# Rows of the second norm moved from GpSimd to VectorE, the exponentials' table loaded earlier, the routing weights computed last

## The chip, the cores and the metric

The kernel runs on one core of one Trainium2 chip. The metric is the device time of one execution in microseconds (us); lower is better. The times shown are the median of several runs, with the lowest and highest.

## What is computed

Two layers of a transformer-like block over 256 latent tokens and 256 context tokens of width 1024, in float32. Each layer runs three token mixers, merges and projects them, and adds the result to the stream. Then comes a second RMS norm with a modulation (a scale and a shift per row kind), a router over 16 experts in 4 groups that picks two experts of one group for each token, and a mixture of gated experts. The first layer keeps context and latents (512 tokens), the second only the latents (256). Cut to the part around the change:

```python
def modulate(h, shift, scale):
    return h * (1 + scale) + shift

mix = token_mixers(h, ...)                      # ends with  merged @ w_out
x = x + m[2] * mix
hx = modulate(rms_norm(x, norm2), m[3], m[4])   # the second norm's rows
probs = softmax(hx @ w_router)
sel = probs + b_router                          # choose group, then two experts
wts = probs[chosen] / sum(probs[chosen])        # the choices' weights
x = x + m[5] * sum(wts * expert(hx))
```

## The kernel before

Each layer is `mixers` followed by `tail` (line 986). `tail` has three stretches.

**Output projection** (`output_projection`, line 903). The merged tiles are split into a rounded high part `mh` (ScalarE, line 913) and the rest `ml` (VectorE, line 914), and each piece of the weights `w_out` into `whi` (ScalarE, line 231) and `wlo` (VectorE, line 232). TensorE makes three matmuls for each block, high by high, high by low, low by high (lines 243 to 245). There are four token tiles of 128 in layer 0 and two in layer 1, and two column halves of 512. `done` evicts a result: times the gate `m2` into `tm` (VectorE, line 921), then added to `x` (line 922). `vectors` (line 1053) issues, from ScalarE's queue behind the last `mh`, the DMAs of the router and the modulation: in layer 0 the 2 MB `m34`, in layer 1 the small `mc8`. `loaded` (line 1067) turns these into what the router needs (columns `mcol`, scaled router `wrm`, bias `blg` by matmuls at line 1081) and scales them: `m34` at line 1087 in layer 0, `mc8` at line 1084 in layer 1.

**Norm and routing.** `tile_done(t)` (line 1091) follows each tile: transposes (line 1098) to `h2T`, the square sum (ScalarE, line 1101), the reciprocal root `rsx` (VectorE and GpSimd, lines 295 and 296), the router's logits (line 1106, `lg` at line 1127). In layer 0 it also makes the norm's rows `xg`: scaled by ScalarE (line 1108), multiplied and shifted by GpSimd in two halves (lines 1111 and 1112), written to `h2d` in DRAM by SyncE's queue (line 1113). In layer 1 it makes a high part `hh` (ScalarE, line 1118) and a low part `hl` of the scaled rows, for tile 0 on VectorE (line 1120) and for tile 1 on GpSimd (lines 1123 and 1124). After each pair of tiles `route` (line 1221) runs: maximum `mx` (line 1228), exponentials `pr` with a load of ScalarE's table (line 1230), reciprocal (line 1233), selection scores `se` (line 1235), the choice of two experts by some twenty small VectorE operations up to `ohb` (line 1267), ranks by matmul (`rnk`, line 1275). What it returns, `weights` (lines 1289 to 1298), makes the normalized weights `wts` and `comb`; it is called last in `tile_done`.

**Placing and experts.** In layer 0 `place_tiles` (line 1302) and `indices` (line 1325) find which row goes to which slot (`M`, `cc`, `gix`, `six`); a gather on GpSimd's queue (line 1371) then reads the rows back from `h2d`, TensorE transposes them (line 1402), and `xh` and `xl` (lines 1403 and 1404) are the first expert's input. In layer 1 `place_group` (line 1339) builds placing masks `Mg` (line 1344), multiplies `hh` and `hl` by them on TensorE (line 1352) and the weights onto the masks (`MW`, line 1363).

The program's text gives dependencies; the order in which each engine issues is set by a scheduler with a cost model, which `tc.issue_after` and `tc.high_priority` steer. So code moved in one place can reorder instructions elsewhere. Every engine issues in its order, one behind the other.

Of the kernel before, what the change touches and what calls it, by code (L numbers as in the profile page):

```python
# [12 lines left out]
F32 = mybir.dt.float32  # L13
# [5 lines left out]
AF = mybir.ActivationFunctionType  # L19
ALU = mybir.AluOpType  # L20
AX = mybir.AxisListType
PSUM = bass.MemoryType.PSUM

D = 1024
NT = 4
# [6 lines left out]
CIDN, CUTR, CIOT, CNCM, CZER, CWAM, CCOS, CSIN, CGD, CED, CPID, CEND = (  # L32
    0, 128, 256, 384, 448, 704, 1216, 1344, 1472, 1476, 1492, 1496)
# [34 lines left out]
def mk(ap, off, dims):  # L68
    return bass.AP(tensor=ap.tensor, offset=ap.offset + off, ap=[list(ap.ap[0])] + [list(d) for d in dims])
# [7 lines left out]
def kernel(es, tc, A, out, dbg=None):  # L77
    nc = tc.nc
    V, S, G, PE, SY = nc.vector, nc.scalar, nc.gpsimd, nc.tensor, nc.sync
# [7 lines left out]
    sm = es.enter_context(tc.tile_pool(name="sm", bufs=2))  # L87
# [38 lines left out]
    C = cst.tile([128, CEND], F32, name="C")  # L126
# [3 lines left out]
    nhalf = cst.tile([128, 8], F32, name="nhalf")  # L130
# [68 lines left out]
    def later():  # L199

        return tc.issue_after(loads[-1].ins)
# [701 lines left out]
    def output_projection(l, op, mg, x, vectors, loaded, tile_done):  # L903

        full = l == 0
        nt = 4 if full else 2
# [4 lines left out]
        for k in range(8):  # L911
            m = mg[k // 4][:, k % 4]
            last = S.copy(mh[:, k], m)
            V.tensor_tensor(ml[:, k], m, mh.bitcast(F32)[:, k], ALU.subtract)

        vectors(last)

        def done(t, dh, ps):
            cs = slice(512 * dh, 512 * dh + 512)
            tm = op.tile([128, 512], F32, name="tm", bufs=2)  # L920
            V.tensor_tensor(tm, ps, m2[:, 1 if full and t < 2 else 0, cs], ALU.mult)
            (V if dh else G).tensor_tensor(x[:, t, cs], x[:, t, cs], tm, ALU.add)
# [59 lines left out]
    h2d = [tc.dram_tile([512, D], F32, name="h2d0")]  # L982
# [3 lines left out]
    def tail(l, mp, mgp, mg, side, other):  # L986


        full = l == 0
        nt = 4 if full else 2  # L990
# [4 lines left out]
        x = xp.__enter__().tile([128, nt, D], F32, name="x")  # L995
# [9 lines left out]
        with ExitStack() as ms, ExitStack() as ps_:  # L1005
            mo = ms.enter_context(tc.tile_pool(name=f"mo{l}", bufs=1, side=side))
            br = mo.tile([128, 16], F32, name="br")
            S.dma_start(br, A["b_router"].partition_broadcast(128))
            utr = mo.tile([128, 128], BF16, name="utr")
            G.tensor_copy(utr, C[:, CUTR:CUTR + 128])  # L1010
            one = mo.tile([128, 128], BF16, name="one")
# [20 lines left out]
            with ExitStack() as rs_:  # L1032
# [17 lines left out]

                lgs, placed = [None], None

# [38 lines left out]
                def tile_done(t):  # L1091
# [13 lines left out]
                    for k in range(8):  # L1105
                        PE.matmul(lg, hT[:, k], wrm[:, r, k], start=k == 0, stop=k == 7)
                    if full:
                        S.activation(xn, x[:, t], AF.Copy, scale=rs)
                        for g in range(2):
                            cs = slice(512 * g, 512 * g + 512)  # L1110
                            G.tensor_tensor(xn[:, cs], xn[:, cs], m34[:, r, 1, cs], ALU.mult)
                            G.tensor_tensor(xn[:, cs], xn[:, cs], m34[:, r, 0, cs], ALU.add)
                        SY.dma_start(h2d[l][128 * t:128 * (t + 1)], xn)
                    else:

                        xk = mk(x, D * t, [[1, 8], [8, 128]])
                        blocks = lambda a: a.rearrange("p (k i) -> p k i", k=8)
                        S.activation(blocks(hh[:, t]), xk, AF.Copy, scale=rs)
                        if t < nt - 1:
                            V.scalar_tensor_tensor(blocks(hl_[:, t]), xk, rs, blocks(hh.bitcast(F32)[:, t]),  # L1120
                                                   ALU.mult, ALU.subtract)
                        else:
                            G.tensor_scalar(blocks(xn), xk, rs, None, ALU.mult)
                            G.tensor_tensor(hl_[:, t], xn, hh.bitcast(F32)[:, t], ALU.subtract)
                    if t % 2 == 0:
                        lgs[0] = rp.tile([128, 2, 16], F32, name="lg", bufs=2)
                    V.scalar_tensor_tensor(lgs[0][:, t % 2], lg, rs, blg[:, r], ALU.mult, ALU.add)
                    if t % 2 == 0:
                        return
                    later = route(rp, lgs[0], t, nt, br, wts, comb, ohb, rnk, rnb if full else None, rhs, utr, one, cnt)  # L1130
                    if full:
                        nonlocal placed
                        placed = place_tiles(rp, (t - 1, t), cap, iot, rnb, rhs, cc, None if t < nt - 1 else
                                    lambda g: indices(rp, cc, gix, six, g))
                    later()

# [15 lines left out]
                if not full:  # L1152
# [7 lines left out]
                    def place(g):  # L1160
                        if g < 4:
                            for a, r in zip((xT, WT), place_group(g, rp, p2, nt, rnk, comb, hh, hl_, mc8)):
                                a.append(r)
# [56 lines left out]

    def route(rp, lg, t1, NT_, br, wts, comb, ohb, rnk, rnb, rhs, utr, one, cnt):

# [4 lines left out]
        bc = lambda x, n, k=1: mk(x, 0, [[k, 2], [0, n]])  # L1227
        V.tensor_reduce(mx, lg, AX.X, ALU.max, negate=True)
        for i in range(2):
            S.activation(pr[:, i], lg[:, i], AF.Exp, bias=mx[:, i:i + 1], accum_out=sm_[:, i:i + 1])  # L1230
        if t1 == NT_ - 1:
# [34 lines left out]
        V.tensor_tensor(o2, e, bc(v, 16), ALU.is_equal)  # L1266
        V.tensor_tensor(ohb[:, t0:t0 + 2], o1, o2, ALU.add)

# [69 lines left out]

    def place_group(g, rp, xp_, nt, rnk, comb, hh, hl_, mc8):

        M = rp.tile([128, nt, 4, 64], F32R, name="Mg", bufs=2)
        xT = xp_.tile([128, 8, 256], F32, name="xT", bufs=2)
        for t in range(nt):
            V.tensor_tensor(M[:, t], mk(C, CIOT, [[0, 4], [1, 64]]), mk(rnk, 16 * t + 4 * g, [[1, 4], [0, 64]]),
                            ALU.is_equal)
        for k2 in range(4):
# [371 lines left out]
```

## Time and profile before

| what | value |
|---|---|
| median of 3 runs | 1770.28 us (1768.99 to 1772.41) |
| the profiled execution | 1766.91 us |
| its span, first to last instruction | 1764.8 us |
| mean granted TensorE clock | 0.976 of full |
| TensorE busy | 1653.8 us, 94% of the span |
| VectorE busy | 1049.4 us, 59% |
| ScalarE busy | 818.7 us, 46% |
| GpSimd busy | 346.2 us, 20% |

Times in the profile count from the span's start. PE is TensorE, DVE VectorE, ACT ScalarE, POOL GpSimd, SP SyncE; a "q" behind a name is the engine's sequencer or queue. A timeline row gives start and duration, engine, line, operation, output and inputs; the bracket at its end is the time that the engine stood idle before it and what ended that. PEclk is the granted clock, 1.00 being the upper of its two levels (2.4 GHz) and 0.50 the lower (1.2 GHz).

### The profile page before, as it was taken

Reading aid. Unit: us, or ns where it says so; the run is one execution under the profiler, and the core shown is the slowest. Engines: PE = TensorE matmul, PEld = TensorE weight load, DVE = VectorE, ACT = ScalarE, POOL = GpSimd, SP = SyncE. Lnnn points to the kernel's source line nnn. Section 1 sums busy time; section 2 is a strip of 40 time slices with the busy share of each in tenths; the row PEclk is TensorE's granted clock in tenths of the full one; section 3 lists DMA queues with packets and bytes.
Section 4 is the critical chain, followed back from the end, with each engine's and each line's share of the span. In section 5 each row is a group of like instructions: output and inputs, shape, how many; then the busy total and the mean of one; then the engine's idle time right before and its main releaser. Section 6 shows DMA issues by size and latency. Waiting matters only on the chain. (4 is left out here: it accounts for less than half of the span.)

```text
span 1764.8 us, 24182 instructions
## 1 busy us (share of the span) xinstructions
PE 1653.8 (94%) x8912; PEld 1218.6 (69%) x8913; DVE 1049.4 (59%) x1908; ACT 818.7 (46%) x1353; POOL 346.2 (20%) x343
## 2 busy tenths in 40 slices
PE   8999999999999999589999996999999999699998
PEld 4657677887677788477877774878887888443333
DVE  4328482447867335688888889488548786411101
ACT  3313232336676442368778774444446875301100
POOL 0003040222300123411221104143213202100000
PEclk9999999999999999799999997999999999899999
DMA  9895747523211355499999962322524345899996
GB/s 289 295 321 175 245 168 257 183 73 96 60 49 36 101 183 196 170 315 368 369 328 364 363 237 86 113 79 60 191 82 105 105 120 204 342 413 414 412 378 269
DMA packets 235312, 380.02 MB, mean 215 GB/s; under 512 B 33447, under 2 KB 130215, under 8 KB 225585
## 3 DMA queue, kind: packets, MB, share of 16 engines
q1 hardware_dynamic: 223248, 361.19, 59.1%
q10 hardware_dynamic: 7616, 9.43, 1.6%
q0 software_dynamic: 4320, 7.75, 1.3%
q8 instruction: 74, 1.21, 0.3%
q14 instruction: 54, 0.43, 0.1%
HBM read 370.50 MB, written 17.72 MB: 220 GB/s over the span
## 5 line engine op out<-in xcount | busy, mean ns | idle before, releaser
L232 DVE TENSOR_TENSOR wlo<-wraw,whi 128x1024 fp32r<-128x1024 f32 (+2 forms) x368 | 438.6, 1212 | 176.1 <-ACT whi L231 161.6
L231 ACT CAST whi<-wraw 128x1024 fp32r<-128x1024 f32 (+2 forms) x368 | 369.4, 1023 | 171.1 <-PE psg L245 77.2
L243 PE MATMUL psg<-hTh,whi 128*128 128x512 f32 (+1 forms) x576 | 206.6, 360 | 0.0
L244 PE MATMUL psg<-hTl,whi 128*128 128x512 f32 (+1 forms) x576 | 205.4, 357 | 0.0
L245 PE MATMUL psg<-hTh,wlo 128*128 128x512 f32 (+1 forms) x576 | 204.2, 356 | 0.0
L243 PE MATMUL psg<-whi,hTh 128*128 128x512 f32 (+1 forms) x392 | 148.6, 383 | 2.2 <-ACT hTh L373 2.1
L244 PE MATMUL psg<-wlo,hTh 128*128 128x512 f32 (+1 forms) x392 | 148.1, 379 | 0.0
L245 PE MATMUL psg<-whi,hTl 128*128 128x512 f32 (+1 forms) x392 | 147.3, 379 | 0.5 <-DVE hTl L404 0.4
L243 PEld LDWEIGHTS psg<-hTh,whi 128*128 128x128 f32 x576 | 109.1, 190 | 27.1 <-issue 10.1
L245 PEld LDWEIGHTS psg<-hTh,wlo 128*128 128x128 f32 x576 | 109.0, 190 | 19.0 <-issue 6.1
L244 PEld LDWEIGHTS psg<-hTl,whi 128*128 128x128 f32 x576 | 109.3, 190 | 16.0 <-issue 4.0
L1478 PE MATMUL psg<-wraw,xT 128*64 128x512 f32 x512 | 113.2, 595 | 2.9 <-PEq L1149 2.7
L243 PE MATMUL psg<-whi,xh 128*128 128x512 f32 x256 | 101.8, 398 | 0.7 <-ACT xh L1403 0.7
L244 PE MATMUL psg<-wlo,xh 128*128 128x512 f32 x256 | 100.0, 391 | 0.0
L245 PE MATMUL psg<-whi,xl 128*128 128x512 f32 x256 | 99.6, 390 | 0.0
L243 PEld LDWEIGHTS psg<-whi,hTh 128*128 128x128 f32 x392 | 74.3, 190 | 19.5 <-ACT hTh L373 3.8
L1478 PEld LDWEIGHTS psg<-wraw,xT 128*64 128x64 f32 x512 | 35.9, 137 | 74.4 <-issue 72.2
L245 PEld LDWEIGHTS psg<-whi,hTl 128*128 128x128 f32 x392 | 73.9, 189 | 16.8 <-DVE hTl L404 1.7
L244 PEld LDWEIGHTS psg<-wlo,hTh 128*128 128x128 f32 x392 | 74.4, 190 | 13.3 <-issue 0.5
L587 ACT ACTIVATE P<-P,smx 128x512 f32<-128x512 f32 (+1 forms) x96 | 62.2, 648 | 22.9 <-DVE smx L586 20.4
L836 POOL TENSOR_TENSOR mg<-mg,gates 128x512 f32<-128x512 f32 (+1 forms) x32 | 38.1, 1198 | 172.1 <-DVE gates L835 126.2
L1371 POOL DMA_INDIRECT xg<-h2d,gix x16 | 27.8, 1739 | 204.5 <-PE pst L1402 188.5
(414 smaller groups left out, 3256.9 us busy)
## 6 DMA issues: line engine op xcount, KB each, us to landing
wraw<-in_w_down_dram SPq DMA_DIRECT2D x64, 1024.0 KB
wraw<-in_w_ada_dram SPq DMA_DIRECT2D x40, 1024.0 KB
wraw<-in_w_in_dram SPq DMA_DIRECT2D x144, 256.0 KB
wraw<-in_w_up_dram SPq DMA_DIRECT2D x32, 1024.0 KB
wraw<-in_w_gate_dram SPq DMA_DIRECT2D x32, 1024.0 KB
wraw<-in_w_gate_dram SPq DMA_DIRECT2D x64, 512.0 KB
wraw<-in_w_up_dram SPq DMA_DIRECT2D x64, 512.0 KB
wraw<-in_w_in_dram SPq DMA_DIRECT2D x24, 1024.0 KB
```

Source lines behind the costliest of these rows:

```text
L231: S.copy(hi[:, :, 0:n], r[:, 2 * j:2 * j + 2, 0:n])
L232: V.tensor_tensor(lo[:, :, 0:n], r[:, 2 * j:2 * j + 2, 0:n], hi.bitcast(F32)[:, :, 0:n], ALU.subtract)
L243: PE.matmul(ps, ah, bh, start=start, stop=False)
L244: PE.matmul(ps, ah, bl, start=False, stop=False)
L245: PE.matmul(ps, al, bh, start=False, stop=stop)
L587: S.activation(flat, flat, AF.Exp, scale=-1.0, bias=m[:, 0:1], accum_out=m[:, 2:3])
L836: G.tensor_tensor(dst, dst, sg[:, i], ALU.add)
L1371: return G.indirect_dma_start(out=xg, out_offset=None, in_=h2d[l][:, :], in_offset=bass.IndirectOffsetOnAxis(ap=idx, axis=0), bounds_check ...
L1478: PE.matmul(pgu[64 * c:64 * c + 64, :], xT[:, 2 * p + k, o:o + 64], r[:, :, k, 256 * c:256 * c + 256], start=p == 0 and k == 0, stop=p == ...
```

## The change

- ScalarE runs one `Exp` on a small tile behind the last `mh` cast of each output projection, so that the table is loaded there (lines 918 and 919 of the changed kernel).
- Layer 0's rows are made on VectorE in two operations of 128x1024: `rows_a` (line 1123) scales by `rsx` and multiplies by `m34`, `rows_b` (line 1131) adds the shift and issues the write. ScalarE's copy and the GpSimd operations are gone. For the last tile `rows_a` is issued behind the maximum, `rows_b` behind the choice.
- In layer 1, for tile 1, GpSimd keeps the scaled rows (now into `xn` first), ScalarE copies them to `hh` behind the exponentials (line 1127), and VectorE subtracts behind the choice (line 1137).
- `weights` runs last: in layer 0 behind the indices, in layer 1 behind the first placing masks.

```diff
@@ output_projection
         vectors(last)
 
+        with tc.issue_after(last.ins):
+            S.activation(sm.tile([128, 8], F32, name="warm"), nhalf, AF.Exp)
+
@@ tail
+                def weigh(after):
+
+                    with tc.issue_after(after.ins):
+                        while weights:
+                            weights.pop(0)()
@@ tile_done
-                    if full:
-                        S.activation(xn, x[:, t], AF.Copy, scale=rs)
-                        for g in range(2):
-                            cs = slice(512 * g, 512 * g + 512)
-                            G.tensor_tensor(xn[:, cs], xn[:, cs], m34[:, r, 1, cs], ALU.mult)
-                            G.tensor_tensor(xn[:, cs], xn[:, cs], m34[:, r, 0, cs], ALU.add)
-                        SY.dma_start(h2d[l][128 * t:128 * (t + 1)], xn)
-                    else:
-
-                        xk = mk(x, D * t, [[1, 8], [8, 128]])
-                        blocks = lambda a: a.rearrange("p (k i) -> p k i", k=8)
-                        S.activation(blocks(hh[:, t]), xk, AF.Copy, scale=rs)
-                        if t < nt - 1:
+
+                    xk = mk(x, D * t, [[1, 8], [8, 128]])
+                    blocks = lambda a: a.rearrange("p (k i) -> p k i", k=8)
+
+                    def rows_a():
+
+                        if full:
+                            V.scalar_tensor_tensor(xn, x[:, t], rs, m34[:, r, 1], ALU.mult, ALU.mult)
+                        elif t < nt - 1:
+                            S.activation(blocks(hh[:, t]), xk, AF.Copy, scale=rs)
+                        else:
+                            S.copy(hh[:, t], xn)
+
+                    def rows_b():
+                        if full:
+                            V.tensor_tensor(xn, xn, m34[:, r, 0], ALU.add)
+                            SY.dma_start(h2d[l][128 * t:128 * (t + 1)], xn)
+                        elif t < nt - 1:
                             V.scalar_tensor_tensor(blocks(hl_[:, t]), xk, rs, blocks(hh.bitcast(F32)[:, t]),
                                                    ALU.mult, ALU.subtract)
                         else:
-                            G.tensor_scalar(blocks(xn), xk, rs, None, ALU.mult)
-                            G.tensor_tensor(hl_[:, t], xn, hh.bitcast(F32)[:, t], ALU.subtract)
+                            V.tensor_tensor(hl_[:, t], xn, hh.bitcast(F32)[:, t], ALU.subtract)
+
+                    if t < nt - 1:
+                        rows_a()
+                        rows_b()
+                    elif not full:
+                        G.tensor_scalar(blocks(xn), xk, rs, None, ALU.mult)
...
-                    later = route(rp, lgs[0], t, nt, br, wts, comb, ohb, rnk, rnb if full else None, rhs, utr, one, cnt)
+                    weights.append(route(rp, lgs[0], t, nt, br, wts, comb, ohb, rnk, rnb if full else None, rhs, utr, one,
+                                         cnt, (rows_a, rows_b) if t == nt - 1 else None))
                     if full:
                         nonlocal placed
                         placed = place_tiles(rp, (t - 1, t), cap, iot, rnb, rhs, cc, None if t < nt - 1 else
                                     lambda g: indices(rp, cc, gix, six, g))
-                    later()
+                    if full and t == nt - 1:
+                        weigh(placed)
@@ route
-        V.tensor_reduce(mx, lg, AX.X, ALU.max, negate=True)
+        first = V.tensor_reduce(mx, lg, AX.X, ALU.max, negate=True)
         for i in range(2):
-            S.activation(pr[:, i], lg[:, i], AF.Exp, bias=mx[:, i:i + 1], accum_out=sm_[:, i:i + 1])
+            second = S.activation(pr[:, i], lg[:, i], AF.Exp, bias=mx[:, i:i + 1], accum_out=sm_[:, i:i + 1])
+        if meanwhile:
+            with tc.issue_after((first if NT_ == NT else second).ins):
+                meanwhile[0]()
...
-        V.tensor_tensor(ohb[:, t0:t0 + 2], o1, o2, ALU.add)
+        chosen = V.tensor_tensor(ohb[:, t0:t0 + 2], o1, o2, ALU.add)
+        if meanwhile:
+            with tc.issue_after(chosen.ins):
+                meanwhile[1]()
@@ place_group
         for t in range(nt):
-            V.tensor_tensor(M[:, t], mk(C, CIOT, [[0, 4], [1, 64]]), mk(rnk, 16 * t + 4 * g, [[1, 4], [0, 64]]),
-                            ALU.is_equal)
+            placed = V.tensor_tensor(M[:, t], mk(C, CIOT, [[0, 4], [1, 64]]), mk(rnk, 16 * t + 4 * g, [[1, 4], [0, 64]]),
+                                     ALU.is_equal)
+        then(placed)
```

The scheduler gives another order in more places than these. Three of them:

VectorE in layer 0's output projection, around the scale of `m34` (the changed kernel's line 1096 is line 1087 before; `wlo` are the splits of `w_out`, numbered by buffer). Before:

```order
L232 TENSOR_TENSOR wlo_5593<-wraw_5526,whi_5592 128x1024
L914 TENSOR_TENSOR ml_5501<-mg_1980,mh_5498 128x512
L232 TENSOR_TENSOR wlo_5597<-wraw_5526,whi_5596 128x1024
L232 TENSOR_TENSOR wlo_5661<-wraw_5528,whi_5660 128x1024
L232 TENSOR_TENSOR wlo_5665<-wraw_5528,whi_5664 128x1024
L921 TENSOR_TENSOR tm_5612<-psg_5540,m2_5499 128x512
L921 TENSOR_TENSOR tm_5627<-psg_5553,m2_5499 128x512
L1087 SCALAR_TENSOR_TENSOR m34_5488<-m34_5488,xg0_5478 128x1024 x2
```

and with the change:

```order
L232 TENSOR_TENSOR wlo_5595<-wraw_5528,whi_5594 128x1024
L914 TENSOR_TENSOR ml_5501<-mg_1980,mh_5498 128x512
L1096 SCALAR_TENSOR_TENSOR m34_5488<-m34_5488,xg0_5478 128x1024
L232 TENSOR_TENSOR wlo_5599<-wraw_5528,whi_5598 128x1024
L232 TENSOR_TENSOR wlo_5663<-wraw_5530,whi_5662 128x1024
L232 TENSOR_TENSOR wlo_5667<-wraw_5530,whi_5666 128x1024
L924 TENSOR_TENSOR tm_5614<-psg_5542,m2_5499 128x512
L924 TENSOR_TENSOR tm_5629<-psg_5555,m2_5499 128x512
L1096 SCALAR_TENSOR_TENSOR m34_5488<-m34_5488,xg0_5478 128x1024
```

The first of the two scales, which waits for the DMA of `m34`, moved ahead of three splits and two evictions.

VectorE in layer 1's output projection, around the scale of `mc8` (line 1084 before, line 1093 in the changed kernel). Before:

```order
L232 TENSOR_TENSOR wlo_14030<-wraw_13953,whi_14029 128x1024
L232 TENSOR_TENSOR wlo_14034<-wraw_13953,whi_14033 128x1024
L921 TENSOR_TENSOR tm_14011<-psg_13965,m2_13924 128x512
L1084 SCALAR_TENSOR_TENSOR mc8_13917<-mc8_13917 128x8
L232 TENSOR_TENSOR wlo_14038<-wraw_13955,whi_14037 128x1024
L921 TENSOR_TENSOR tm_14026<-psg_13978,m2_13924 128x512
L232 TENSOR_TENSOR wlo_14042<-wraw_13955,whi_14041 128x1024
L1073 COPY mcol_13906<-pst_14045 128x8 x2
```

and with the change:

```order
L1093 SCALAR_TENSOR_TENSOR mc8_13907<-mc8_13907 128x8
L232 TENSOR_TENSOR wlo_14022<-wraw_13945,whi_14021 128x1024
L924 TENSOR_TENSOR tm_14003<-psg_13957,m2_13914 128x512
L232 TENSOR_TENSOR wlo_14026<-wraw_13945,whi_14025 128x1024
L232 TENSOR_TENSOR wlo_14030<-wraw_13947,whi_14029 128x1024
L924 TENSOR_TENSOR tm_14018<-psg_13970,m2_13914 128x512
L232 TENSOR_TENSOR wlo_14034<-wraw_13947,whi_14033 128x1024
L1082 COPY mcol_13896<-pst_14037 128x8 x2
```

The scale, which waits for the DMAs of `mc8`, moved ahead of two splits and one eviction.

VectorE in layer 0 behind the last pair's maximum `mx`; the reciprocal (line 1233 before, 1257 in the changed kernel) is the last pair's, the operations with `_5874` to `_5876` (`_5870` to `_5872` with the change) and the first `ohb` are the first pair's. Before:

```order
L1228 TENSOR_REDUCE mx<-lg 128x2
L1253 TENSOR_TENSOR e<-a_5874,v 128x32
L1254 TENSOR_TENSOR e<-e,C 128x32
L1255 TENSOR_REDUCE v<-e 128x2
L1266 TENSOR_TENSOR o_5876<-e,v 128x32
L1267 TENSOR_TENSOR ohb<-o_5875,o_5876 128x32
L1279 TENSOR_SCALAR rhs<-o_5876 128x2x16
L1292 TENSOR_TENSOR o_5875<-pr,o_5875 128x32
L1292 TENSOR_TENSOR o_5876<-pr,o_5876 128x32
L1293 TENSOR_REDUCE w<-o_5875 128x2
L1233 RECIPROCAL sme<-sme 128x2
```

and with the change:

```order
L1249 TENSOR_REDUCE mx<-lg 128x2
L1123 SCALAR_TENSOR_TENSOR xg_5478<-x,rsx,m_5488 128x1024
L1257 RECIPROCAL sme<-sme 128x2
L1277 TENSOR_TENSOR e<-a_5870,v 128x32
L1259 SCALAR_TENSOR_TENSOR se<-pr,sme,br 128x16 x2
L1278 TENSOR_TENSOR e<-e,C 128x32
```

The reciprocal moved from behind the first pair's choice to directly behind the last tile's first row pass; the two chains now alternate.

## Rows read from the trace of the kernel before

**Rows 1.** The page's busy times: engine, busy us (share of the span), instructions.

```profile
PE 1653.8 (94%) x8912; PEld 1218.6 (69%) x8913; DVE 1049.4 (59%) x1908; ACT 818.7 (46%) x1353; POOL 346.2 (20%) x343
```

**Rows 2.** Windows: us, then busy us of PE, PEld, DVE, ACT, POOL.

```profile
720.00:730.00 10.00, 4.09 (x21) 3.02 (x20) 8.09 (x32) 6.57 (x11) 3.46 (x4) 0.79 0.63 215
1510.00:1520.00 10.00, 1.69 (x12) 1.40 (x13) 4.60 (x18) 6.74 (x10) 6.74 (x3) 0.72 1.03 408
```

**Rows 3.** VectorE's timeline, layer 0's hole.

```profile
717.78 2.18 DVE L1235 SCALAR_TENSOR_TENSOR se<-pr,sme,br 128x16 f32<-128x16 f32 x2
...
726.86 0.19 DVE L1228 TENSOR_REDUCE mx<-lg 128x2 f32<-128x32 f32 x1
...
732.28 0.15 DVE L1233 RECIPROCAL sme<-sme 128x2 f32<-128x2 f32 x1
...
732.48 0.38 DVE L1235 SCALAR_TENSOR_TENSOR se<-pr,sme,br 128x16 f32<-128x16 f32 x2
...
746.67 0.16 DVE L1334 TENSOR_TENSOR gix<-I,J 128x8 uint32<-128x8 f32 x1
...
754.98 1.43 DVE L1404 TENSOR_TENSOR xl<-pst,xh 128x512 fp32r<-128x512 f32 x2 [2.03 <-ACT xh L1403]
```

**Rows 4.** GpSimd's timeline, both holes.

```profile
717.39 2.54 POOL L1112 TENSOR_TENSOR xg<-xg,m 128x512 f32<-128x512 f32 x2
...
727.09 2.48 POOL L1111 TENSOR_TENSOR xg<-xg,m 128x512 f32<-128x512 f32 x2 [1.26 <-ACT xg L1108]
...
1512.34 3.84 POOL L1123 TENSOR_SCALAR sq<-x,rsx 128x1024 f32<-128x1024 f32 x1
```

**Rows 5.** ScalarE's timeline, layer 0's projection and layer 1's hole.

```profile
669.52 1.05 ACT L231 CAST whi<-wraw 128x1024 fp32r<-128x1024 f32 x1 [4.78 <-DMA mrow<-m_dram]
...
1514.42 1.28 ACT L1230 ACT_TABLE_LOAD   x1
```

**Rows 6.** VectorE's timeline, layer 1's hole.

```profile
1513.04 0.19 DVE L1228 TENSOR_REDUCE mx<-lg 128x2 f32<-128x32 f32 x1
...
1516.64 2.14 DVE L1235 SCALAR_TENSOR_TENSOR se<-pr,sme,br 128x16 f32<-128x16 f32 x2
```

**Rows 7.** GpSimd's timeline, layer 0's experts, line 1452.

```profile
866.49 5.75 POOL L1452 TENSOR_SCALAR M<-C,rnk 128x128 f32<-128x128 f32 x4
911.64 2.86 POOL L1452 TENSOR_SCALAR M<-C,rnk 128x128 f32<-128x128 f32 x4 [7.67 <-PE pst L1454]
```

**Rows 8.** VectorE's timeline around the scales, both output projections.

```profile
679.93 3.36 DVE L1087 SCALAR_TENSOR_TENSOR m<-m,xg 128x1024 f32<-128x1024 f32 x2 [0.33 <-DMA m<-m_dram]
...
1491.30 0.17 DVE L1084 SCALAR_TENSOR_TENSOR mc<-mc 128x8 f32<-128x8 f32 x1 [1.94 <-DMA mc<-in_norm_dram]
1491.39 1.22 DVE L232 TENSOR_TENSOR wlo<-wraw,whi 128x1024 fp32r<-128x1024 f32 x1
...
1494.26 0.23 DVE L1073 COPY mcol<-pst 128x8 f32<-128x8 f32 x2
```

**Rows 9.** TensorE's timeline, both output projections.

```profile
661.44 0.40 PE L243 MATMUL psg<-whi,mh 128*128 128x512 f32 x1
...
676.15 0.63 PE L244 MATMUL psg<-wlo,mh 128*128 128x512 f32 x2
...
1491.31 0.40 PE L244 MATMUL psg<-wlo,mh 128*128 128x512 f32 x1
...
1494.59 0.36 PE L1081 MATMUL pst<-wr,mcol 128*128 128x16 f32 x2
```

**Rows 10.** DMA queues, 669 to 680: packets, MB, share of 16 engines.

```profile
q10 hardware_dynamic: 309, 2.20, 51.2%
q1 hardware_dynamic: 906, 1.82, 47.0%
```

**Rows 11.** SyncE's queue, 716 to 756, the last tile's write.

```profile
732.03 0.34 SPq L1113 DMA_DIRECT2D h2d<-xg  x1
```

**Rows 12.** GpSimd's queue at the gather's line: ns min/median/max, first and last start.

```profile
L1371 POOLq EVENT_SEMAPHORE  x5: 17/43/11639, 729.7 to 755.2; - x5
```

More of the change, by code (lines that the diff above doesn't have):

```diff
@@ L1049, in tail @@
                 blg = rp.tile([128, len(rr), 16], F32, name="blg")
-                lgs, placed = [None], None
+                lgs, placed, weights = [None], None, []
+                def weigh(after):
+                    with tc.issue_after(after.ins):
+                        while weights:
+                            weights.pop(0)()
                 def vectors(last):
@@ L1161, in place @@
                         if g < 4:
-                            for a, r in zip((xT, WT), place_group(g, rp, p2, nt, rnk, comb, hh, hl_, mc8)):
+                            for a, r in zip((xT, WT), place_group(g, rp, p2, nt, rnk, comb, hh, hl_, mc8, weigh)):
                                 a.append(r)
@@ L1219, in tail, with route @@
         return xp, x, rest
-    def route(rp, lg, t1, NT_, br, wts, comb, ohb, rnk, rnb, rhs, utr, one, cnt):
+    def route(rp, lg, t1, NT_, br, wts, comb, ohb, rnk, rnb, rhs, utr, one, cnt, meanwhile):
         t0 = t1 - 1
@@ L1337, in indices, with place_group @@
         return V.tensor_tensor(six[:, e], I, K, ALU.add)
-    def place_group(g, rp, xp_, nt, rnk, comb, hh, hl_, mc8):
+    def place_group(g, rp, xp_, nt, rnk, comb, hh, hl_, mc8, then):
         M = rp.tile([128, nt, 4, 64], F32R, name="Mg", bufs=2)
```

## The prediction

> **What bounds the kernel now.** I read the page's busy shares first: TensorE is busy 94% of the span [rows 1]. So a change to anything else pays only where TensorE stands idle. The windows show where: in 720 to 730 TensorE works 4.09 of 10 us, in 1510 to 1520 only 1.69 of 10, while VectorE works 8.09 and 4.60 [rows 2]. These two holes lie between the output projection and the experts of each layer. There the second norm, the router, the top-2 choice and the placing of tokens run one behind the other, mostly on VectorE. What shortens a hole, or lengthens the projection ahead of it, moves the end by as much, since at 94% TensorE has hardly any slack elsewhere.
>
> Next I read VectorE's timeline through layer 0's hole [rows 3]. The last pair's maximum is ready at 727.05 (726.86 + 0.19), but its reciprocal runs at 732.28. No transfer lies between: VectorE is held up on the first pair's chain. The timeline of GpSimd says by what [rows 4]: the row adds run in 717.39 to 719.93, the next tile's multiplies from 727.09 on. Two `se` beside the first of these took 2.18 us, two without GpSimd 0.38 [rows 3]. So two-input work on GpSimd holds up two-input work on VectorE. The hole ends with `gix` at 746.67, the gather behind it and the first `xl` at 754.98 [rows 3].
>
> **The parts, against the profiled execution.** It took 1766.91 us (span 1764.8), 3.37 under the median of 1770.28. The sum is a difference, so I add it to the median.
>
> *Warm table load.* One `Exp` on 8 columns and one load, 1.28 us [rows 5], per layer. In layer 0 it falls right ahead of a cast before which ScalarE sat idle 4.78 us [rows 5], and the matmul that needs that cast's split runs at 676.15 [rows 9]: cost 0, and so I take it in layer 1, where the load stands ahead of the cast in the same place. What it saves is counted under layer 1's hole.
>
> *Layer 0's hole.* Four scaled copies on ScalarE and sixteen GpSimd operations of 1.25 us each (2.54 us for two, [rows 4]) go; four 128x1024 pairs on VectorE come. The nearest VectorE row for such a pass is a split, 1.22 us [rows 8]. Those of tiles 0 to 2 fall in gaps between evictions; they cost 0 while VectorE has such gaps, up to 2.4 us a tile if one is too short. For tile 3 the first pass stands behind the maximum, so the reciprocal can run at 727.05 + 1.2 = 728.25: 4.0 earlier. The second pass stands behind the choice and adds 1.2. The weights' operations leave the path to `gix`, which I put at 0.6 (six of 0.1). `gix` comes 4.0 - 1.2 + 0.6 = 3.4 earlier, near 743.3. Late next is VectorE behind `gix`: both pairs' weights (twenty small operations, about 0.11 apart, 2.2 us) and four splits (4.9) now stand ahead of `xl`, with the second half's indices about 1.4, 8.5 us in all against 8.3 from `gix` to `xl` in before. That gives back 0.4. **Term: -3.0**; bounds -4.4 (the second pass hidden) and +0.8 (the row write, see the rivals).
>
> *Layer 1's hole.* The maximum ends at 1513.23 [rows 6]; ScalarE, behind its copy to `hh`, loads the table at 1514.42 [rows 5] and has it at 1515.70, for the exponentials. Now nothing stands between, so they start 2.5 earlier and the reciprocal can run near 1514.0. But GpSimd's strided scaling stays, 1512.34 to 1516.18 [rows 4]. If it holds up `se` (two inputs) until it ends, the pair of `se` ends at 1516.6 instead of 1518.78 [rows 6]: -2.2. If not, -4.2. No row has this pair of operations side by side. The maximum beside it was not slowed (0.19), but it reads one tensor. Nearest is another single-tensor GpSimd operation, the scaling of `iota` at L1452: four took 5.75 us under VectorE's splits and 2.86 in another place [rows 7]. So such an operation does exclude a two-input one, and I take -2.2.
>
> The Trainium skill, "SBUF — State Buffer", section "SBUF: two separate sides", says that a VectorE operation with two SBUF inputs and a GpSimd operation that reads SBUF exclude each other for a whole instruction. By that rule `se` waits for 1516.18 and this part is -2.2; without it the sum would be 2.0 lower.
>
> The subtraction of 128x1024 moves to VectorE behind the choice: 1.2, like a split, some of it inside the wait for the rank matmul. Against it the weights between the two placing masks and four transposes ahead of the first expert leave the path. I put the two together at +0.2, between +1.2 (neither helps) and +0.2. **Term: -2.0**; bounds -4.0 (`se` free) and -1.0.
>
> *Layer 0's projection.* The reordering has a price that the diff does not show. The scale of m34 needs a 2 MB transfer that in before was waited for until 679.93 [rows 8]. There it stood behind three splits; now it stands ahead of them. VectorE works in order, so the split that TensorE needs next sits behind a transfer. TensorE's 64 matmuls from 661.44 to 676.15 come every 0.23 us [rows 9]; by the new order the blocked split is first read after 72 of them, at 678.2. Landing plus one scale (1.2) plus one split (1.2) give 682.3 if the landing stays at 679.93: a stall of 4.2. The landing can move: in 669 to 680 the queue of this transfer moved 2.20 MB beside 1.82 MB of weights [rows 10], and most of those weights are issued later when the splits are. With half of them (4.0 MB became 3.1 MB, or 8.5 us from 669) it lands near 677.6: a stall of 1.9. **Term: +2.0**, nearer to the second since the cause (fewer transfers beside it) is certain; bounds 0 (landed by 675.8) and +4.2.
>
> *Layer 1's projection.* The same with the scale of mc8, which waited 1.94 us for its DMA until 1491.30 with two splits and an eviction already done [rows 8]. Now these stand behind it too. From 1491.39, split, eviction, split took to 1494.26, 2.87 us [rows 8]; twice that, and the column copies start at 1497.1 instead of 1494.26. TensorE reads the first of these splits at 1491.31 and stands at the router's bias matmuls at 1494.59, which need the columns [rows 9]. It stalls 1.2 at the split (ready at 1492.5) and is 2.9 late at the bias. **Term: +2.9**; bounds +1.2 and +3.5. The landing itself has no reason to move.
>
> **Sum:** -3.0 - 2.0 + 2.0 + 2.9 = -0.1, so 1770.2. What the holes gain the projections lose. A measurement of this kernel tells about 0.2% (3.5 us) from no change, so this is no change.
>
> **The rivals.** *The waits cost little, faster.* If m34 lands by 675.8 and mc8 costs the lower bound, the sum is -3.0 - 2.0 + 0 + 1.2 = -3.8, 1766.5; with a free `se` -5.8, 1764.5; with every low end -4.4 - 4.0 + 0 + 1.2 = -7.2, 1763.1. For it: fewer transfers run beside m34's. Against: DMA engines were never idle in that stretch, and mc8's wait is measured. Chance 0.30.
>
> *The row write is late, slower.* Tile 3's rows must be in DRAM before the gather. In before the write was issued at 732.03 and GpSimd's queue waited 11.64 us from 729.7, to 741.3 [rows 11, 12], perhaps for it: up to 9.2 us behind weight loads. This was covered, as `gix` came at 746.67. Now the write is issued only behind the second pass, near 738.4, with four weight loads ahead of it on SP's queue instead of two. It decides from a landing of 743.3 on. With 9.2 us again it lands at 747.6, 0.8 behind the end of `gix` in before (746.83), and the first term turns to +0.8: +0.8 - 2.0 + 2.0 + 2.9 = +3.7, 1774.0; with m34 at its upper end 1776.2. For it: 1 MB loads in a row. Against: those loads are issued near 724, so most are through by 738; the wait may have been for something else. Chance 0.25.
>
> *The moved work hides nothing.* If the holes end with the gather's or weights' own waits, the terms shrink together and the time is 1770 to 1773; this is part of the middle case.
>
> **How the numbers follow.** No change 0.45, faster 0.30, slower 0.25. These are the chances of below, within and above 0.2%. The range takes the likeliest and reaches to the low ends of the faster case (1763.1) and the top of the slower (1776.2), less a bit at each end: 1763.5 to 1775.5. The likeliest case's own range is 1767 to 1773.
>
> **What would show it.** Right: VectorE waits for m34 with splits queued behind it and TensorE has a gap of about 2 us near 678; the same near 1491 with the bias matmuls some 3 us later than before relative to the last gate merge; the last pair's reciprocal 1.2 us behind its maximum; in layer 1 the exponentials right behind the maximum, but `se` stretched to the end of GpSimd's scaling. Wrong: no gap near 678 (the transfer landed in time, then faster); or the gather's idle time ended by the row write, not by `gix` (then slower).

## The result, and the profile after

The changed kernel takes 1783.53 us (median of 5 runs, 1778.70 to 1787.24) against 1771.08 us for the kernel before beside it: ratio 1.006, 95% interval 1.0035 to 1.0085. A second comparison, of the same two kernels, gave 1.0052 (1.0034 to 1.007). So it is slower by 0.5 to 0.6%, 9 to 11 us, and outside the predicted range. The profiled execution took 1787.24 us, span 1785.3, the slowest of its five; a second profile of the changed kernel (below) took 1778.69.

The page's busy times answer [rows 1]: TensorE's instructions are the same, 8912, but they took 16 us longer.

```profile
PE 1670.0 (94%) x8912; PEld 1233.8 (69%) x8913; DVE 1047.7 (59%) x1917; ACT 812.9 (46%) x1351; POOL 324.6 (18%) x326
```

VectorE's timeline of the changed kernel from layer 0's projection to its first expert answers [rows 3, 8]:

```profile
678.25 1.23 DVE L1096 SCALAR_TENSOR_TENSOR m<-m,xg 128x1024 f32<-128x1024 f32 x1 [10.49 <-DMA m<-m_dram]
679.39 3.49 DVE L232 TENSOR_TENSOR wlo<-wraw,whi 128x1024 fp32r<-128x1024 f32 x3
...
738.36 0.18 DVE L1249 TENSOR_REDUCE mx<-lg 128x2 f32<-128x32 f32 x1
738.47 1.28 DVE L1123 SCALAR_TENSOR_TENSOR xg<-x,rsx,m 128x1024 f32<-128x1024 f32 x1
739.66 0.16 DVE L1257 RECIPROCAL sme<-sme 128x2 f32<-128x2 f32 x1
...
753.60 0.16 DVE L1361 TENSOR_TENSOR gix<-I,J 128x8 uint32<-128x8 f32 x1
...
766.66 1.29 DVE L1432 TENSOR_TENSOR xl<-pst,xh 128x512 fp32r<-128x512 f32 x2 [4.38 <-ACT xh L1431]
```

The reciprocal follows the maximum by 1.3 us instead of 5.4 [rows 3]: what the change is for works. But VectorE stood 10.49 us for `m34` with three splits queued behind, and from `gix` to `xl` it takes 13.06 us instead of 8.31 [rows 3]. TensorE's timeline shows both ends of that, and layer 1's pauses (answers [rows 9]):

```profile
680.66 0.50 PE L244 MATMUL psg<-wlo,mh 128*128 128x512 f32 x1 [2.57 <-DVE wlo L232]
...
682.08 0.63 PE L245 MATMUL psg<-whi,ml 128*128 128x512 f32 x1
...
685.11 0.40 PE L243 MATMUL psg<-whi,mh 128*128 128x512 f32 x1
...
762.61 1.94 PE L1430 MATMUL pst<-C,xg 128*128 128x128 f32 x8 [7.77 <-DVEq L1170]
...
1506.43 0.49 PE L244 MATMUL psg<-wlo,mh 128*128 128x512 f32 x1 [1.18 <-DVE wlo L232]
1510.39 0.49 PE L244 MATMUL psg<-wlo,mh 128*128 128x512 f32 x1 [0.56 <-DVE wlo L232]
1512.32 0.81 PE L1090 MATMUL pst<-wr,mcol 128*128 128x16 f32 x6 [1.43 <-issue]
```

The same 128x512 matmul takes 0.63 us at 682 and 0.40 at 685. The windows of the changed kernel say why (3 us each: busy us of PE, PEclk, DMA share, GB/s):

```profile
682.00:685.00 3.00, 3.00 (x9) 0.56 0.90 331
...
697.00:700.00 3.00, 3.00 (x8) 0.50 0.02 6
...
724.00:727.00 3.00, 3.00 (x13) 0.50 0.43 175
727.00:730.00 3.00, 3.00 (x9) 0.50 0.00 0
...
1515.00:1518.00 3.00, 3.00 (x8) 0.50 1.03 419
1518.00:1521.00 3.00, 3.00 (x12) 0.50 1.03 412
1521.00:1524.00 3.00, 3.00 (x10) 0.50 1.02 406
```

TensorE works without a pause there; at 0.50 that is at 1.2 GHz. In layer 1, 9 us at 0.50 cost 4.5 us of work (an estimate: half of the stretch). The kernel before has low windows in layer 0 too, but fewer, and ran layer 1's projection at 1.00 throughout:

```profile
691.00:694.00 3.00, 3.00 (x11) 0.63 0.29 104
694.00:697.00 3.00, 3.00 (x12) 0.80 0.00 0
...
1483.00:1509.00 26.00, 25.15 (x134) 1.00 0.97 346
```

I cut each profile into five stretches, from VectorE's and TensorE's timelines: **P0**, layer 0's projection, from the last `ml` to the last `tm`; **H0**, last `tm` to first `gix`; **B0**, first `gix` to `xl`; **P1**, layer 1's projection (as P0); **H1**, last `tm` to the first expert's first matmul. Each is taken from start to start, in us, from one profile of each kernel.

| kernel | ratio to before (95%) | P0 | H0 | B0 | P1 | H1 |
|---|---|---|---|---|---|---|
| before | | 54.83 | 24.45 | 8.31 | 25.18 | 22.86 |
| before, again (e8) | 0.9992 (0.9974, 1.001) | 56.36 | 24.48 | 8.03 | 25.07 | 23.62 |
| **changed** | 1.006 (1.0035, 1.0085) | 66.04 | 20.48 | 13.06 | 33.65 | 19.80 |
| **changed, again (e13)** | 1.0052 (1.0034, 1.007) | 60.79 | 20.46 | 13.84 | 30.62 | 19.80 |
| e1 changed, scales pinned | 1.0015 (1.0001, 1.0029) | 60.65 | 19.66 | 13.19 | 26.96 | 19.44 |
| e2 before + warm load | 1.0056 (1.003, 1.0081) | 61.30 | 22.76 | 8.11 | 30.58 | 22.65 |
| e3 before + late weights | 1.0034 (1.0019, 1.005) | 57.98 | 24.11 | 12.96 | 25.19 | 23.79 |
| e4 e1 + early weights | 0.9986 (0.9972, 1.0) | 56.07 | 20.96 | 8.84 | 25.47 | 19.97 |
| e5 before + warm, pinned | 1.0017 (0.9998, 1.0036) | 59.05 | 22.32 | 8.11 | 25.40 | 22.03 |
| **e6 rows alone** | 0.997 (0.9955, 0.9986) | 54.82 | 23.06 | 7.43 | 25.14 | 20.30 |
| e7 changed, early weights | 1.003 (1.0018, 1.0043) | 61.23 | 21.78 | 8.62 | 29.19 | 19.51 |
| e9 e6 + early scales | 1.0043 (1.0023, 1.0063) | 61.07 | 22.50 | 7.44 | 30.45 | 20.38 |
| e10 e11, `mc8` early | 1.0023 (1.001, 1.0037) | 57.67 | 20.93 | 9.14 | 32.39 | 20.29 |
| e11 e6 + warm, pinned | 0.9992 (0.9977, 1.0008) | 59.05 | 20.96 | 9.07 | 25.45 | 20.31 |
| **e12 e6 pinned** | 0.9956 (0.9941, 0.9971) | 54.81 | 22.85 | 7.41 | 25.22 | 21.60 |
| e14 e12, last pair late | 1.0003 (0.9986, 1.002) | 59.58 | 21.29 | 13.33 | 25.14 | 21.46 |

The holes win what they should (H0 -4.0, H1 -3.1). P0, B0 and P1 lose 11.2, 4.8 and 8.5 in this profile; 6.0, 5.5 and 5.4 in the second.

P0 varies by itself. The two profiles of the changed kernel differ in it by 5.2 us; so do e12 and e14 by 4.8 and e4 and e11 by 3.0, though in each pair TensorE and VectorE run this stretch in the same order. A difference of 5 us in P0 between two single profiles therefore shows nothing; the pauses in it, and the times of several runs, do.

### The profile page after: what moved, and what is told of

Same layout as the page of the kernel before. It is cut to its first block, busy times and chain, and to the rows that moved or that the text cites. A ratio compares the mean times of both kernels' runs of the same rounds, so it can differ in the third digit from the quotient of the medians.

```text
span 1785.3 us, 24163 instructions
## 1 busy us (share of the span) xinstructions
PE 1670.0 (94%) x8912; PEld 1233.8 (69%) x8913; DVE 1047.7 (59%) x1917; ACT 812.9 (46%) x1351; POOL 324.6 (18%) x326
## 5 line engine op out<-in xcount | busy, mean ns | idle before, releaser
L243 PEld LDWEIGHTS psg<-whi,hTh 128*128 128x128 f32 x392 | 74.5, 190 | 19.4 <-ACT hTh L373 3.8
```

Source lines behind the costliest of these rows:

```text
L243: PE.matmul(ps, ah, bh, start=start, stop=False)
```

## The experiments

Theory: the warm load makes the scheduler put the scales ahead of the splits, which costs in both projections (A), and late weights put work ahead of the branches, which costs in B0 (C). The rivals B and D say that the loss lies elsewhere.

**e1, the changed kernel with both scales behind an eviction of the first column half, as before.** The edit ("pinning" from here on):

```diff
-                        for r in rr:
-                            V.scalar_tensor_tensor(m34[:, r, 1], m34[:, r, 1], 1.0, n2, ALU.add, ALU.mult)
+                        with tc.issue_after(evicted.ins):
+                            for r in rr:
+                                V.scalar_tensor_tensor(m34[:, r, 1], m34[:, r, 1], 1.0, n2, ALU.add, ALU.mult)
```

`mc8` likewise; `evicted` is the second `tm` of the projection in layer 0, the first in layer 1.

> The changed kernel, with the scales of m34 and mc8 held behind the first evictions, where the kernel before had them; everything else of the change stays. Theory A (the two scales ahead of the splits stall TensorE and pull its granted clock down behind the stall): layer 0's projection loses its stall of 2.6 us near 678 and the half-clock stretches behind it, layer 1's its stalls of 3.2 us and the half-clock stretch; in the profile up to 19 us less than the changed kernel's 1785.3, in the median 1766 to 1772. Rival B (the projections are slow because VectorE now makes the rows, or because of the table load itself): at most the 2.6 and 3.2 us of waiting go and the half clock stays, 1777 to 1781.

1773.53 us. TensorE's pauses behind the splits are gone and P1 is 26.96. That is 1.5 us above A's range and 3.5 below B's: A, with some of the loss left. P0 (60.65) still has its stretches at the lower clock.

**e2, the kernel before with the `warm` lines of the change and nothing else.**

> The kernel before, with nothing but the early Exp added. By its order that alone moves both scales ahead of the splits. Theory A: both projections get the stalls and half-clock stretches of the changed kernel, 8 to 19 us, less 1 to 2 us for the table load that leaves layer 1's hole: 1777 to 1788. Rival B: the projections stay as before and the table load's 1.3 us are gained: 1768 to 1771.

1780.93 us: one `Exp` on eight columns costs nearly as much as the whole change. P0 and P1 carry it (61.30, 30.58).

**e3, the kernel before with layer 0's weights last.**

```diff
-                    later()
+                    if not full:
+                        later()
+                    else:
+                        weights.append(later)
+                        if t == nt - 1:
+                            weigh(placed)
```

> The kernel before, with layer 0's weights computed last and nothing else. By its order that alone puts four splits instead of two ahead of VectorE's branch and a weight load, which waits for one of them, ahead of SyncE's branch. Theory C (the engines' first instructions behind the branch wait for the others' branches): TensorE's transposes start at the end of VectorE's branch and not at the gather's landing, and ScalarE's copy xh waits for SyncE; the first xl comes 3 to 5 us later against gix, some of it paid by an earlier gix (0.5 to 1): 1773 to 1776. Rival D (the weights are off the path and only the gather counts): 1769 to 1771.

1776.67 us; B0 grows from 8.31 to 12.96. C, 0.7 us above its range.

**e4, e1 with layer 0's weights computed where the kernel before does.**

```diff
-                    if full and t == nt - 1:
-                        weigh(placed)
+                    if full:
+                        while weights:
+                            weights.pop(0)()
```

> The changed kernel with the scales held back as in e1, and layer 0's weights computed behind each pair's placing as in the kernel before. Theories A and C: e1 less the 4 to 5 us that the branch costs, so layer 0's gain up to gix reaches xl: 3 to 5 us under e1, 1762 to 1767, faster than the kernel before. Rivals B or D: no faster than e1.

1768.90 us, above the range. B0 is back (8.84), the holes are 6.4 us shorter than before, yet the time hardly fell. Something else still costs.

**e5, e2 with the scales pinned.**

> The kernel before with the warm exponential added, but the two scales (m34, mc8) held behind the evictions of the output projection's first half, as the kernel before orders them. Theory (the load costs nothing; all of the 11.8 us of the run with the warm load alone came from the scales' new place): no pause of TensorE of over 1 us behind the splits in either projection, layer 1's projection (last ml to last tm) 25 to 27 us instead of 30.6 to 33.7, layer 1's first exponentials right behind the maximum, time 1767 to 1771 us, ratio 0.998 to 1.001. Rival (the load itself, or the traffic around it, costs time): 1776 us or more with the scales in their old place.

1771.88 us, 0.9 above the theory's range and 4 below the rival's. P1 is back at 25.40, P0 is not (59.05). The ratio's interval holds 1, so this alone does not decide whether the load is free.

**e6, the rows off GpSimd alone: the changed kernel without the warm lines, both layers' weights where they were.**

> Only the rows move off GpSimd (scalar_tensor_tensor and additions on VectorE); no warm load, both layers' weights where the kernel before has them. Theory: layer 0's gix comes 3 to 4 us earlier behind the last tm, the step from gix to the last xl stays at 8 to 9 us (before 8.31), layer 1 wins 1 to 2 us less than with the table loaded early; projections as before; by the sum 1764 to 1767 us, and as the run with pinned scales and early weights gave back most of its 6 us, 1765 to 1770 us is what I take. Rival (the rows on VectorE cost as much as they win): 1770 to 1773 us, with the gix no earlier.

1765.66 us, at the low end and faster than before. `gix` comes only 1.4 us earlier, short of the 3 to 4 expected: the weights stay ahead of it. But H1 (20.30) is nearly as short as with the warm load (19.4 to 20.0 in e1, e4 and the changed kernel). In e6 ScalarE loads the table at 1511.89, right behind the square sum, and then still waits 0.73 us for the maximum. The same shows in e12, which has the same rows:

```profile
1508.57 0.19 ACT L1110 ACTIVATION_READ_ACCUMULATOR sq<-x 128x1 f32 x1
1508.77 1.28 ACT L1255 ACT_TABLE_LOAD   x1
1511.56 0.31 ACT L1255 ACTIVATE pr<-lg,mx 128x16 f32<-128x16 f32 x1 [1.50 <-DVE mx L1253]
```

Since ScalarE's strided copy no longer stands behind the square sum, the table is loaded while ScalarE waits for the maximum. Layer 1's load was hidden by the rows' move; the warm load had nothing to add there.

**e7, the changed kernel with e4's edit and free scales.**

> The changed kernel with layer 0's weights computed where the kernel before does; the scales stay early. Theory (two separate losses: the scales' place in both projections, and the weights and splits ahead of VectorE's branch): the step from gix to the last xl falls from 13.1 to 8 to 9 us, the projections stay long (layer 1's 30 to 34 us), time 1775 to 1781 us, that is 3 to 6 us under the changed kernel. Rival (weights last costs nothing when the rest is there): 1782 to 1786 us.

1775.69 us. B0 falls to 8.62; the pauses of 2.45 and 1.18 us in the projections stay.

**e8, the kernel before again.**

> The kernel before, word for word, once more: what its own profile varies by. Ratio 0.998 to 1.002. If layer 0's projection (last ml to last tm) is 54.8 us again, the profile of before is typical, and the 58 to 61 us of the runs with the old order of the scales are costs of their edits; if it is 56 to 61 us, that stretch varies by itself by as much with where TensorE's granted clock falls, and only layer 1's projection and the pauses can be compared between single profiles.

1769.22 us. P0 is 56.36, 1.5 us above the first profile; P1 and B0 agree to 0.3. That is the expectation's second case: P0 varies with where the clock falls.

**e9, e6 with early scales and no warm load.**

```diff
-                        V.scalar_tensor_tensor(mc8[:, 0], mc8[:, 0], 1.0, mc8[:, 2], ALU.add, ALU.mult)
+                        with tc.high_priority():
+                            V.scalar_tensor_tensor(mc8[:, 0], mc8[:, 0], 1.0, mc8[:, 2], ALU.add, ALU.mult)
```

`m34` likewise.

> The kernel of the run with the rows alone, without any warm load, but the scales m34 and mc8 given a high priority, so that they stand on VectorE ahead of splits that they stood behind: both m34 ahead of the last two pairs of splits of layer 0, mc8 one split earlier than in the changed kernel's place. Theory (the place of the scales alone makes the loss, the warm load only moves them): a pause of TensorE of over 1 us on a split in layer 0's projection and a longer projection there (58 to 64 us), layer 1's 27 to 33 us; 1770 to 1778 us. Rival (the loss needs the load itself): both projections as in the rows-only run (54.8 and 25.1 us) and 1764 to 1768 us.

1776.92 us, 11 above e6's 1765.66. VectorE's timeline in layer 0, and TensorE's:

```profile
677.53 2.36 DVE L1095 SCALAR_TENSOR_TENSOR m<-m,xg 128x1024 f32<-128x1024 f32 x2 [8.69 <-DMA m<-m_dram]
679.81 1.28 DVE L921 TENSOR_TENSOR tm<-psg,m 128x512 f32<-128x512 f32 x2
681.01 4.17 DVE L232 TENSOR_TENSOR wlo<-wraw,whi 128x1024 fp32r<-128x1024 f32 x2
```

```profile
682.99 0.50 PE L244 MATMUL psg<-wlo,mh 128*128 128x512 f32 x1 [1.11 <-DVE wlo L232]
685.23 0.50 PE L244 MATMUL psg<-wlo,mh 128*128 128x512 f32 x1 [0.57 <-DVE wlo L232]
689.35 0.84 PE L1087 MATMUL pst<-wr,mcol 128*128 128x16 f32 x6 [1.88 <-DVE mcol L1079]
```

The place of the scales alone makes the loss: the pauses sum to 3.6 us here, and P0 grows by 6.3, P1 by 5.3. The bias matmuls, whose columns come later too, pause the longest.

**e10, all weights early, `m34` pinned, `mc8` free, warm load in; e11, the same with both pinned; e12, e6 with both pinned and no warm load.**

> Rows off GpSimd, warm load in, all weights early, m34 held behind the evictions as before, and only layer 1's mc8 left where the warm load brings it, ahead of splits. Theory (each projection pays about half): layer 1's projection 29 to 34 us with a pause of 1.2 us, layer 0's without a pause of over 1 us; 4 to 7 us above the run with both pinned, that is 1769 to 1773 us. Rival (layer 0's scale makes nearly all of it): within 2 us of the run with both pinned.

> Rows off GpSimd, warm load in, both scales pinned, all weights early: the two gains without the two losses. Theory of the holes alone: layer 1's hole 19.5 to 20.5 us as in the rows-only run, layer 0's exponentials no later; 1763 to 1767 us, the same as the rows-only run. Rival (the warm load, or pinning, costs 3 to 4 us that the holes do not show, as the two earlier pinned runs hint): 1767 to 1771 us.

> The rows-only kernel with the scales pinned and no warm load; VectorE's order in the projections is that of the rows-only run, only TensorE's order behind the scales can differ. If pinning itself costs (layer 0's projection 58 us and more by another order of TensorE's small matmuls): 1768 to 1771 us. If it does not: 1764 to 1767 us, and what the earlier pinned runs lack comes from the warm load.

e10 1775.77, e11 1770.04, e12 1764.78 us on one chip. Layer 1's scale costs 5.7 us (P1 32.39 against 25.45), which the layer 1 half of the theory foresaw. e11's rival holds: with the scales pinned the load still costs 5.3 us, and pinning itself none. The two profiles are only 2.4 us apart (1767.21 and 1764.78). P0, 59.05 against 54.81, shows a part. TensorE at the bias matmuls, of e12 and of e11:

```profile
685.97 3.69 PE L1088 MATMUL pst<-wr,mcol 128*128 128x16 f32 x32
```

```profile
687.27 3.75 PE L1091 MATMUL pst<-wr,mcol 128*128 128x16 f32 x32 [0.92 <-DVE mcol L1083]
```

Both kernels have the two passes of `m34` ahead of the last two splits. But in e11 the load delays the casts behind it by 1.9 us (668.32 in e11, 667.17 in e12, the last `ml` at 665.17 and 665.87), TensorE's matmuls stand in another order, and the eviction behind which the passes are pinned comes 13.2 us behind the last `ml` instead of 11.5. So the columns come later, TensorE pauses 0.92 us, and the bias matmuls start 22.1 us behind the last `ml` instead of 20.1. These 2.0 us show in all five kernels with the load in and `m34` pinned (e1, e4, e5, e10, e11). The rest of P0's difference is a second stretch at the lower clock, which e12 does not have (windows of e11):

```profile
715.00:718.00 3.00, 3.00 (x13) 0.51 0.22 89
718.00:721.00 3.00, 3.00 (x10) 0.50 0.21 86
```

**e13, the changed kernel again.**

> The changed kernel, word for word, once more. Time 1780 to 1786 us. If the first profile is typical: layer 0's projection 64 to 67 us with 35 or more slow 128x512 matmuls, layer 1's 32 to 34 us. If stretches at half clock fall by chance on top of the pause: the pause of 2.5 us and layer 1's 1.2 us stay, but layer 0's projection comes to 60 to 63 us and layer 1's to 29 to 31 us, as in the other kernels with early scales.

1779.06 us, 0.9 under the range. The second case: the pauses are there (3.29 and 1.16 us), P0 is 60.79 and P1 30.62. Of the first profile's 11.2 us in P0 some 5 are a stretch at the lower clock, 721 to 733, that this one does not have.

**e14, e12 with only the last pair's weights behind the indices.**

```diff
-                    if full:
-                        while weights:
-                            weights.pop(0)()
+                    if full and t == nt - 1:
+                        weigh(placed)
+                    elif full:
+                        weights.pop(0)()
```

> The kernel with the rows moved and the scales pinned (no warm load), but the last pair's weights of layer 0 behind the indices; by that four splits instead of two, and SyncE's load of a gate piece, stand ahead of the branches. Theory (the splits and the load ahead of the branches are the loss): layer 0's ohb to gix falls from 8.9 to under 7 us, gix to the last xl rises from 7.4 to 11 us and more, together 1 to 4 us longer than 16.3 us; 1765.5 to 1769 us. Rival (only the number of small operations behind the index counts, here one pair's instead of two): gix to the last xl under 9.5 us, 1762 to 1765 us.

1773.01 us, above both. `ohb` to `gix` falls from 8.9 to 7.3 us, short of the under 7 expected, and B0 rises to 13.33. VectorE is done with the weights at 754.91. TensorE's transposes and `xh`, of e14, and the transposes of e12:

```profile
756.23 1.94 PE L1435 MATMUL pst<-C,xg 128*128 128x128 f32 x8 [8.01 <-DVEq L1175]
759.71 1.07 ACT L1436 CAST xh<-pst 128x512 fp32r<-128x512 f32 x2 [26.99 <-DMA h2d<-xg]
```

```profile
749.08 1.94 PE L1434 MATMUL pst<-C,xg 128*128 128x128 f32 x8 [4.32 <-DMA xg<-h2d,gix]
```

In e12 the transposes wait for the gather and start 5.6 us behind `gix`; in e14 they wait for VectorE's queue and start 9.2 behind it. `xh` follows them by 1.2 us in e12 and by 3.5 in e14. The row write that its bracket names was issued at 741.04 and read back before the transposes, so it is not what `xh` waits for. Its start points to SyncE, whose queue issues its next load at 759.74. SyncE's waits (line, waited for: us, times, longest), of e14 and of e12:

```profile
SPq L215 <- DVE wlo L232: 8.2, 1, 8.2
SPq L1175 <- SPq L1175: 6.6, 2, 5.5
```

```profile
SPq L1174 <- SPq L1174: 4.9, 1, 4.9
...
SPq L215 <- DVE wlo L232: 0.4, 1, 0.4
```

A load of a gate piece needs the buffer that a split frees. In e14 it stands ahead of SyncE's branch and waits 8.2 us for VectorE; only then come the branch's own 5.5 us. In e12 it stands behind the branch. The changed kernel's waits are those of e14:

```profile
SPq L215 <- DVE wlo L232: 7.6, 1, 7.6
SPq L1170 <- SPq L1170: 5.5, 1, 5.5
```

and its ScalarE says who waits for that:

```profile
766.05 1.07 ACT L1431 CAST xh<-pst 128x512 fp32r<-128x512 f32 x2 [25.26 <-SPq L1170]
```

So of the 5.9 us by which B0 is longer, VectorE's queue makes 3.7 and SyncE's 2.2 on top; the rival, which counts small operations alone, allowed under 9.5 to the last `xl`. What of it either queue would cost without the other is not shown. The rest of e14's 8 us over e12 lies by the profile in P0 (59.58), at the lower clock without any early scale.

**The account**, at 1770 us: the rows win 5 to 8 us (e6, e12). The early scales cost 6.5 to 8 with the load in (e2 against e5, e1 against the changed kernel), the load beyond that 3 to 6 (e5, whose interval holds 1, and e11 against e12), layer 0's late weights 4 to 6 (e3, e7 against the changed kernel). Layer 1's late weights show no cost (e4 against e11, which differ in them alone: 0.9986 and 0.9992). With the middles, -6.5 + 7.2 + 4.5 + 5 = +10, against 9 to 11 measured. The split between scales and load holds for this order only: e9 loses 11 us by the scales without any load. e12, the rows alone, beats both kernels.

## Why the prediction was wrong

- **Layer 0's hole, -3.0: fell at the 0.4 given back.** `gix` came 4.0 us earlier relative to the last `tm` (forecast 3.4), the reciprocal right behind the row pass as said. But I added up what VectorE does between `gix` and `xl` and did not ask what else `xh` waits for. VectorE's sum itself came out: it was done 8.7 us behind `gix` (forecast 8.5). But in the kernel before TensorE's transposes waited for the gather:

```profile
753.11 1.94 PE L1402 MATMUL pst<-C,xg 128*128 128x128 f32 x8 [5.20 <-DMA xg<-h2d,gix]
```

  In the changed kernel they waited for VectorE's queue and started 9.0 us behind `gix` instead of 6.4, and `xh` followed them by 3.4 us instead of 1.2, waiting for SyncE's. I named that queue only for the row write. Together this is the 4.8 us that B0 grew by, and the stretch from the last `tm` to `xl` ended 0.8 longer than before. The 0.4 was also a slip: 8.5 against 8.3 is 0.2.
- **The row write as the slower rival: did not happen.** GpSimd's gather waited for VectorE's index operations at 754.06; the write had been issued at 749.22. Slower came by another way than the one to which I gave 0.25.
- **Layer 1's hole, -2.0: right in kind, too small** (-3.1). The step that failed is the assumption that GpSimd's strided scaling holds up `se`. The changed kernel's GpSimd and VectorE:

```profile
1534.79 3.84 POOL L1143 TENSOR_SCALAR sq<-x,rsx 128x1024 f32<-128x1024 f32 x1
```

```profile
1537.01 0.38 DVE L1259 SCALAR_TENSOR_TENSOR se<-pr,sme,br 128x16 f32<-128x16 f32 x2
```

  `se` took 0.38 us in the middle of that operation, as long as without GpSimd [rows 3]. The Trainium skill, "SBUF — State Buffer", section "SBUF: two separate sides", would have them exclude each other; for this single-tensor operation of GpSimd the trace does not agree. The spread in [rows 7], my nearest row, is then no evidence for it; its cause stays open. The gain was also booked to the wrong edit: e6 has it without the warm load.
- **Layer 0's projection, +2.0, and layer 1's, +2.9: mechanism right, size wrong.** `m34` landed at 678.25 (estimate 677.6), TensorE paused 2.57 (1.9); in layer 1 1.18 (1.2). But P0 grew by 6.0 to 11.2 and P1 by 5.4 to 8.5. In layer 0 the bias matmuls started 4.2 to 4.9 us later behind the last `ml` than in the kernel before; the rest is the clock, which varies there by itself. In P1 of the first profile the pauses of 1.18, 0.56 and, at the bias matmuls, 1.43 us (at 1512.32) leave 5.3 of the 8.5, and three windows at 0.50 are 4.5 of these. I costed the work behind a pause at the clock that it had before. e10 shows layer 1's part as 5.7 us of time; my bound was 3.5.
- **Warm load, 0: right for ScalarE, wrong for the kernel.** No matmul waits for the casts that the load delays, but it changes the order of the others, and even with the scales pinned it costs 3 to 6 us; 2.0 of them show as the later bias matmuls.
- **The range.** The large errors had one sign, and none of my bounds had room for a clock that falls or for a second queue at the branch. So the top end, 1775.5, was 4 to 8 us short of the two medians (1779.06, 1783.53).

Still open is what decides the second low stretch in P0. With the load in and `m34` pinned it came in e1, e5 and e11 but not in e4 and e10; it came without any load in e3 and e14, and in only one of the two profiles of the changed kernel. The loss of e11 against e12 is shown as a time (10 runs against 5); that this stretch makes what it has beyond the 2.0 us is not shown.

## What to carry to other kernels

Where a scheduler sets the order, compare the orders of each edit alone: one small activation here moved two waiting scales ahead of splits and cost more than the rows won. Never let an operation that waits for a DMA stand, on an in-order engine, ahead of what feeds TensorE, and cost a pause of TensorE above its own length. At a branch look at every engine's queue: work left ahead of VectorE's branch, and a load ahead of SyncE's that waits for a buffer, hold up whoever waits for these queues.

## What the runs showed of the hardware

- TensorE ran at the lower clock while fully busy, in stretches behind pauses or small matmuls. In layer 1 each kernel with an early `mc8` had some (changed: 1515 to 1524 at 0.50); of the others only e1 had one, 1509 to 1512 at 0.52, and e12 had none:

```profile
1483.00:1507.00 24.00, 22.58 (x123) 1.00 0.98 356
```

  A pause alone does not bring it: behind the changed kernel's 2.57 us in layer 0 the clock was 0.56 in 682 to 685, but e13's 3.29 us in the same place left it at 1.00 until 691.
- At the branch the engines do not all wait for the same one. In the changed kernel TensorE's transposes followed VectorE's branch (762.61); ScalarE's `xh` waited for SyncE's, 3.4 us later.
- A GpSimd operation with one tensor input, strided, 3.84 us, did not slow VectorE operations with two inputs inside it (two in 0.38 us).
